# The merge of three branches by features, and chosen remainders for the places of tiles

## The chip, the cores and the metric

The kernel runs on one core of one Trainium2 chip. The metric is the device time of one execution in microseconds. Three runs of the kernel before gave 543.06, 543.06 and 543.47 us, so the median is 543.06 us.

## The reference

One decoder block over 256 positions of 1,024 features, in fp32. A normalised input `h` goes through one wide matrix `w_in`, whose columns feed three token mixers side by side: an attention with compressed, selected and windowed keys (NSA, 16 heads of 64), a chunked linear recurrence (mLSTM, 4 heads of 128) and an attention over 256 fixed memory tokens (4 heads of 128). Three more stretches of 1,024 columns are gates. The branches are merged, projected, normalised and added; a SwiGLU mixer with 2,816 hidden features follows.

```
gm = jax.nn.sigmoid(g_merge.reshape(B, S, N_BRANCH, D_MODEL))
y = (gm[:, :, 0] * (y_nsa @ w_proj_nsa[l]) + gm[:, :, 1] * (y_ml @ w_proj_ml[l])
     + gm[:, :, 2] * (y_mem @ w_proj_mem[l]))
x = x + rmsnorm(y @ w_out[l], g_post_mix[l])
h = rmsnorm(x, g_pre_ffn[l])
gu = h @ w_ffn_in[l]
gate, up = gu[..., :D_FF], gu[..., D_FF:]
x = x + rmsnorm((jax.nn.silu(gate) * up) @ w_ffn_down[l], g_post_ffn[l])
```

## The kernel before

**Split operands.** Each fp32 operand of the large products is split into two parts, `hi` (rounded by the scalar engine, ACT) and `lo` (what is left, by the vector engine, DVE); `split` does it. A product is three matmuls: hi·hi, hi·lo, lo·hi (`mm3`). Weights arrive by DMA in 161 units of 128 x 1,024 fp32 into four buffers `raw`, and `parts` splits each into `whi` and `wlo`, four buffers each. One unit feeds 6,144 streamed columns: 12 matmuls of 512 or 24 of 256.

**Two ways to multiply.** In a matmul one operand is *held* in the array (128 columns, loaded by a weight load) and the other is *streamed* through it.
- *Features-major* (`fmaj`, `fpair`): the weights are held, the activations streamed, 256 columns (the positions) a matmul. The result has features on partitions and tokens along the row. The held tile is used in the order hi, hi, lo and the streamed one in the order hi, lo, hi.
- *Tokens-major* (`tmaj`): the activations are held, the weights streamed, 512 columns a matmul; the result has tokens on partitions.
- `fcat` (gate and up projections of the channel mixer): the weights are held; seven matmuls stream `hi` and `lo` of the activation together, 512 columns, with `hi` weights, then eight stream 256 columns with `lo` weights, then the eighth of 512.

**Stages.** Memory keys and values (`mem_k`, `mem_v`, from the tiles `mh`, `ml`); the normalised input into `hh`, `hl`; keys and values of NSA (`kv`); the small gates (`pgf`); memory attention; then four NSA groups (`nsa_queries`, `nsa_half`), among which other work is placed as filler by the list `ORDER`: `q` and `s` (mLSTM queries and keys), `v`, `g`, `h` (heads), `f`, and six `m`. Each `m` is a `merge_half`: half of the columns of one gate, tokens-major, copied from PSUM into `gm`. After the last group comes the merge. For each half of the features and each branch it takes the sigmoid of `gm`, multiplies the projection in PSUM with it and adds the products in the tile `mrg` on DVE. The sum has tokens on partitions, and `w_out` needs features there, so sixteen transposes of 128 x 128 on the matrix engine bring it to PSUM (`pty`), and `split` writes `yh` and `yl`. Then `w_out`, the first four hidden tiles by `ffn_gate` and `ffn_up` tokens-major, the rest by `fcat`, and `ffn_down`, which holds `u0` to `u5`.

**The order of the work.** Nothing is issued as it is written down. Each operation is recorded with its dependencies (`Plan.record`) and an estimated cost (`cost`); `schedule` lists them onto the engines, `replay` times the list, and `choose` tries two values of a matmul's surcharge, two of slack, and 40 random changes, and keeps the shortest. All DMAs go through the queue of SyncE (SP).

**Where tiles lie.** A tile has its address, in bytes along the partition, from the order in which pools and tags come into use; nothing is chosen. The addresses of the compiled program before, modulo 0x100:

| tile (tag) | used as | address, remainder |
|---|---|---|
| `xc` and the NSA keys `kk` (KK) | streamed | 0x7ac0: 0xc0 |
| `mh`, `u0`, a gate (G, first) | streamed / held | 0xbcc0: 0xc0 |
| `ml`, `u2`, a gate (G, second) | streamed / held | 0xdcc0: 0xc0 |
| `u1`, a gate (G, third) | held | 0x1bd00: 0 |
| `vs`, `u5`, a `wq` (V) | held / streamed | 0xfd00: 0 |
| `ymem`, `yml`, two more (E) | held | 0x11d00, 0x13d00: 0 |
| `hh`, `hl`, later `yh`, `yl` | streamed and held | 0x15d00, 0x17d00: 0 |
| `kmem`, `ynh`, `ynl`, `u3`, `u4` (Y) | streamed / held | 0x1dd00, 0x1fd00: 0 |
| `qs`, `qm` (qs) | held | 0x21d00, 0x22d00: 0 |
| `whi`, `wlo` (four each) | held and streamed | 0x23d00 and on: 0 |
| `pTh`, `pTl` (pT0, pT1) | streamed | 0x33ee0, 0x34f00: 0xe0, 0 |
| `vcs` (held), `ce0`, `ce1` (streamed) | | 0x7240: 0x40; 0x36100, 0x36b00: 0 |

All instructions carry line 598 in the profile, the line that issues the recorded operations, so groups are told apart by the names of tiles.

Of the kernel before, what the change touches and what calls it, by code (L numbers as in the profile page):

```python
# [168 lines left out]
class Plan:  # L169
# [67 lines left out]
    @staticmethod  # L237
    def cost(op):

        n = op.outs[0].n if op.outs else 0  # L240
        views = op.outs + op.ins
        sources = [v for v in op.ins if not v.tile.psum and v.n > 1]
        wide = op.method in ("tensor_copy", "tensor_scalar") and not any(v.tile.psum for v in op.outs)
        op.port = op.eng == "POOL" and bool(op.ins) or op.eng == "DVE" and len(sources) > 1 - wide
        op.load = 0.0
        if op.dma:
            n = views[0].n * 4
            return views[0].shape[0] * n / (230.0 if n < 2048 else 400.0)
        if op.eng == "PE":
            dtype = op.a[1].dtype  # L250
            op.load = 56.0 if dtype == BF16 else 109.0
            if op.method == "transpose":
                return n / 1.2 + 2
            if dtype == F32:
                return max(1.72 * op.a[1].n, n / 0.6 + 10)
            return n / 2.4 + (2.5 if dtype == BF16 else 13.3) + (100 if op.a[1].shape[0] <= 32 else 0)
        n = max(v.n for v in views)
        psum = any(v.tile.psum for v in views)
        pointers = sum(v.n == 1 for v in op.ins)
        part = any(v.place() != (0, P) and v.shape[0] >= 32 for v in op.outs + [v for v in op.ins if v.n > 1])  # L260
# [12 lines left out]
        return 100 + 1.4 * n if op.method == "tensor_scalar" else max(150.0, 2.1 * n - 70)  # L273
# [80 lines left out]
    def schedule(self, matmul, slack, boost):  # L354
# [50 lines left out]
        while len(order) < len(ops):  # L405
# [123 lines left out]

    MATMUL, SLACK, PASSES, ROUNDS = (10.0, 13.3), (60.0, 130.0), 3, 40  # L530

    def choose(self):
# [51 lines left out]
        return self.schedule(matmul, slack, boost)  # L584

    def issue(self):
        order = self.choose()
# [3 lines left out]
        arg = lambda x: x.real() if isinstance(x, View) else x  # L591
        with self.tc.manual_schedule():
            for op in order:
# [4 lines left out]
                op.ins_ = getattr(op.real, op.method)(*map(arg, op.a), **{k: arg(x) for k, x in op.kw.items()})  # L598
# [3 lines left out]
def block_kernel(ctx, tc, order, xN, xT, memN, head, cst, vec, row, wg, w1, w2, W, out):  # L602
# [55 lines left out]

    def parts(raw, into=None):
        hi, lo = into or [wpool.tile([P, 1024], F32R, tag=t, bufs=4, name=t) for t in ("whi", "wlo")]  # L660
        split(hi, lo, raw)
        return hi, lo

    def unit(key, into=None):
        if key not in ready:
            fetch(key)
        return parts(ready.pop(key), into)

# [13 lines left out]
    def fcat(xc, w, ps):  # L682


        hi, lo = unit(w)
        b = lambda k: slice(k * P, (k + 1) * P)
# [13 lines left out]

    def tmaj(xs, *key, n=4, ps_new=ps_d, into=None, last=0):

# [13 lines left out]
        for u in range(n - last):  # L716
            w = unit((*key, u))
            for tb in range(2):
                use(u, tb, w)
        us = range(n - last, n)  # L720
        ws = [unit((*key, u), into and into[u]) for u in us]
        for tb in range(2):
# [61 lines left out]
    wgt = work.tile([P, 1024], F32, tag="p", bufs=2, name="wgt")  # L784
    w2t = one.tile([P, 192], F32, name="w2t")
    part(0, 776)
# [9 lines left out]
    for u in range(4):  # L796
        if u and ("mem_k", u) not in ready:
            fetch(("mem_k", u))
        raw = ready.pop(("mem_k", u)) if u else mt[:, 264:1288]
        w = [wpool.tile([P, 1024], F32R, tag=t, bufs=4, name=t) for t in ("whi", "wlo")]  # L800
        pieces = HEAD[u]
# [38 lines left out]

    vps = tmaj(M, "mem_v", ps_new=ps_s)
    with plan.later(60):
# [30 lines left out]

    hid = one.tile([P, 2, NG, 32], F32, name="hid")
    POOL.memset(hid, 0.0)
    for j in range(2):
# [20 lines left out]
        bias = work.tile([P, 1], F32, tag="b1", bufs=2, name="cbias")  # L897
        DVE.tensor_copy(bias, ph[:, 64:65])
# [198 lines left out]
    def ml_head(h):  # L1097
# [60 lines left out]

    gm = [bigt("G", 3, [P, 2, D], F32, f"gm{b}") for b in range(3)]
# [121 lines left out]
    yl = bigt("hl", 1, [P, 8, S], F32R, "yl")  # L1281
    for h in range(2):
        c = slice(512 * h, 512 * h + 512)
        m = [work.tile([P, 1024], F32, tag="p", bufs=2, name="mrg") for _ in range(2)]
        for b, name, xs, n in ((1, "proj_ml", yml, 2), (2, "proj_mem", ymem, 2), (0, "proj_nsa", (ynh, ynl), 4)):
            g2 = gm[b][:, :, c]
            ACT.activation(g2, g2, AF.Sigmoid, after=last_exp)
            for tb, ps in enumerate(tmaj(xs, name, h, n=n, ps_new=ps_ds, last=2)):
                acc, new = m[tb][:, 0:512], m[tb][:, 512:1024]
                if b == 1:  # L1290
                    DVE.tensor_mul(acc, ps, gm[b][:, tb, c])
                else:
                    DVE.tensor_mul(new, ps, gm[b][:, tb, c])
                    DVE.tensor_add(acc, acc, new)
# [128 lines left out]
def _layout(inputs):  # L1423
# [110 lines left out]
```

## Time and profile before

| | |
|---|---|
| median of three runs | 543.06 us |
| span of the profiled execution, first to last instruction | 540.7 us |
| what lies around it (543.06 − 540.7) | 2.4 us |
| matrix engine busy | 530.9 us, 3,116 matmuls |
| DVE busy | 414.2 us |
| ACT busy | 340.8 us |
| mean granted clock of the matrix engine | 0.999 |
| DMA | 97.85 MB, mean 181 GB/s |

The profile is one execution on the chip. A row that groups instructions gives the busy time, the mean length of one and the idle time of the engine ahead of them. Matmuls are pipelined and the ends of their rows are modelled, so lengths overlap (a matmul of 512 columns is shown as 389 ns long while the next one begins 227 ns after it). What a matmul costs in a run without waits is therefore read from one start to the next.

### The profile page before, as it was taken

What the parts mean: (1) busy time and instruction counts of PE and PEld (TensorE: products, weight loads), DVE (VectorE), ACT (ScalarE), POOL (GpSimd) and SP (SyncE); (2) the same over time, 40 slices, a digit from 0 to 9 for tenths busy, and PEclk for the clock granted to TensorE, in tenths of its full rate; (3) what the DMA queues carried; (4) which work ended last, traced back from release to release, by engine and by line L of the source; (5) the groups of instructions that cost most, each with busy time, mean ns of one, the idle gap of its engine ahead of it and who ended that gap; (6) DMA issues with size and microseconds to landing.
All of it is one profiled execution on the core that took longest, in us unless ns stands there. A gap on an engine that the chain in (4) does not pass through costs nothing.

```text
span 540.7 us, 8802 instructions
## 1 busy us (share of the span) xinstructions
PE 530.9 (98%) x3116; PEld 464.9 (86%) x3116; DVE 414.2 (77%) x900; ACT 340.8 (63%) x682; POOL 30.2 (6%) x43
## 2 busy tenths in 40 slices
PE   9999999999999999999999999999999999999995
PEld 9899998998989889888888888788888888888884
DVE  6795696799999998997987796965777777754543
ACT  7695695566688885966895435744555556653431
POOL 0110000010010111101120000000000000000000
PEclk9999999999999999999999999999999999999999
DMA  8995346525433264254455474834455555555512
GB/s 317 416 412 188 129 136 195 183 79 199 146 137 128 88 234 155 98 177 155 149 174 187 167 257 159 272 118 156 166 190 189 193 196 195 189 187 191 190 63 78
DMA packets 28699, 97.85 MB, mean 181 GB/s; under 512 B 3312, under 2 KB 5232, under 8 KB 28400
## 3 DMA queue, kind: packets, MB, share of 16 engines
q1 hardware_dynamic: 28656, 97.30, 50.6%
q8 instruction: 24, 0.39, 0.3%
q14 instruction: 19, 0.16, 0.1%
HBM read 95.19 MB, written 1.05 MB: 178 GB/s over the span
## 4 chain that ended last, share of the span: by engine, by line
PE 79%; DVE 9%; ACT 5%; DMA 4%; issue 2%; POOL 1%; SPq 0%; DVEq 0%; ACTq 0%
PE pd L598 41%; PE pss L598 27%; DMA raw<-in_W 4%; DVE wlo L598 2%; PE pvn L598 2%; PE sc L598 2%; ACT whi L598 1%; PE ptn L598 1%; PE ph L598 1%; DVE cy L598 1%; ACT L598 1%; DVE sc L598 1%; DVE xt L598 1%; PE psm L598 1%; PE pgf L598 1%
## 5 line engine op out<-in xcount | busy, mean ns | idle before, releaser
L598 DVE TENSOR_TENSOR wlo<-raw,whi 128x1024 fp32r<-128x1024 f32 (+1 forms) x159 | 191.7, 1210 | 83.8 <-ACT whi L598 82.4
L598 ACT ACTIVATE whi<-raw 128x1024 fp32r<-128x1024 f32 (+1 forms) x159 | 166.2, 1051 | 128.8 <-PE pd L598 64.7
L598 PE MATMUL pd<-hh,whi 128*128 128x256 f32 x208 | 59.4, 286 | 0.9 <-DVE on L598 0.9
L598 PE MATMUL pd<-hh,wlo 128*128 128x256 f32 x208 | 59.5, 286 | 0.0
L598 PE MATMUL pd<-hl,whi 128*128 128x256 f32 x208 | 59.2, 285 | 0.0
L598 PE MATMUL pd<-whi,hh 128*128 128x512 f32 x144 | 57.7, 400 | 0.0
L598 PE MATMUL pd<-wlo,hh 128*128 128x512 f32 x144 | 57.5, 399 | 0.0
L598 PE MATMUL pd<-whi,hl 128*128 128x512 f32 x144 | 57.0, 398 | 0.0
L598 PE MATMUL pss<-xc,whi 128*128 128x512 f32 x168 | 43.6, 395 | 0.0
L598 PE MATMUL pss<-whi,u 128*128 128x512 f32 x132 | 42.0, 390 | 0.0
L598 PEld LDWEIGHTS pd<-hh,whi 128*128 128x128 f32 x208 | 39.7, 191 | 1.3 <-DVE on L598 1.1
L598 PEld LDWEIGHTS pd<-hh,wlo 128*128 128x128 f32 x208 | 39.8, 191 | 0.0
L598 PEld LDWEIGHTS pd<-hl,whi 128*128 128x128 f32 x208 | 39.7, 191 | 0.1
L598 PEld LDWEIGHTS pss<-xc,whi 128*128 128x128 f32 x168 | 30.5, 188 | 5.6
L598 PE MATMUL pd<-xc,whi 128*128 128x512 f32 x120 | 32.2, 397 | 0.0
L598 PEld LDWEIGHTS pd<-whi,hl 128*128 128x128 f32 x144 | 27.1, 188 | 4.4
L598 PEld LDWEIGHTS pd<-whi,hh 128*128 128x128 f32 x144 | 27.1, 188 | 4.4 <-ACT cx L598 0.3
L598 PEld LDWEIGHTS pd<-wlo,hh 128*128 128x128 f32 x144 | 27.1, 188 | 4.3 <-DVE wlo L598 0.3
L598 DVE CUSTOM_DVE_ANT_0 sc<-sc,msk 128x16 f32<-128x16 f32 (+2 forms) x96 | 27.2, 316 | 4.2 <-PE sc L598 3.4
L598 PEld LDWEIGHTS pss<-whi,u 128*128 128x128 f32 x132 | 24.8, 188 | 5.3
L598 ACT ACTIVATE pp<-sc,mx 128x128 f32<-128x128 f32 (+1 forms) x64 | 26.7, 427 | 1.5 <-DVE mx L598 1.3
L598 PE MATMUL pss<-wlo,u 128*128 128x512 f32 x66 | 25.8, 390 | 0.0
(333 smaller groups left out, 1122.0 us busy)
## 6 DMA issues: line engine op xcount, KB each, us to landing
raw<-in_W SPq DMA_DIRECT2D x161, 512.0 KB, 3.4
w<-in_w SPq DMA_DIRECT2D x2, 1024.0 KB, 8.1
xn<-in_xN SPq DMA_DIRECT2D x2, 512.0 KB, 9.8
xt<-in_xT SPq DMA_DIRECT2D x2, 512.0 KB, 8.2
mn<-in_memN SPq DMA_DIRECT2D x2, 512.0 KB, 8.8
kk<-kk SPq DMA_DIRECT2D x8, 128.0 KB, 3.1
x<-in_xN SPq DMA_DIRECT2D x2, 512.0 KB, 3.8
memt<-in_head SPq DMA_DIRECT2D x1, 512.0 KB, 6.4
```

The costliest lines, as they stand in the source:

```text
L598: op.ins_ = getattr(op.real, op.method)(*map(arg, op.a), **{k: arg(x) for k, x in op.kw.items()})
```

## The change

The merge and its gates are computed features-major. `gm` holds features on partitions; a gate comes from `fpair` (12 pairs of feature tiles in the place of six halves tokens-major), the projections from `fmaj`, in four pairs of feature tiles. The sum `acc` then lies as `w_out` needs it, and `split` reads it from SBUF. The weights of the gates and projections are laid out in features-major units by the host; there are 161 units as before.

`lay_out` gives tiles their places: for each pool in turn it takes the tags in the order of `RESIDUE`, adds a pad so that the tag's place has the wanted remainder modulo 0x100, and allocates all other tags behind. `whi` and `wlo` become 1,088 columns wide, and a unit starts 0, 32 or 48 columns into them (0, 0x80 or 0xc0 bytes): 0 for features-major products, 48 for tokens-major ones (0 for `mem_v` and for those units of `ffn_down` that meet `u` tiles in G and V), and 32 for the `hi` part of `fcat`. To make room, `w2t` and `hid` share the tiles `ce0` and `ce1`, `cbias` has one buffer, and the unused result of the mLSTM squares goes to a part of `msk` that is not read any more.

The planner's costs of a plain matmul change from n/2.4 + 13.3 (less 0 or 3.3) to n·17/38.4 + 1.5 (less 0 or 3.0), and it tries 100 random changes instead of 40.

```diff
-            return n / 2.4 + (2.5 if dtype == BF16 else 13.3) + (100 if op.a[1].shape[0] <= 32 else 0)
+            return (n / 2.4 + 2.5 if dtype == BF16 else n * 17 / 38.4 + 1.5) + (100 if op.a[1].shape[0] <= 32 else 0)
...
-                        cost += matmul - 13.3
+                        cost += matmul
...
-    MATMUL, SLACK, PASSES, ROUNDS = (10.0, 13.3), (60.0, 130.0), 3, 40
+    MATMUL, SLACK, PASSES, ROUNDS = (-3.0, 0.0), (60.0, 130.0), 3, 100
...
+    FIRST_BYTE = 0x4080
+    RESIDUE = {"vcs": 0, "V": 0, "C": 0, "G": 0, "qs": 0, "KK": 0xC0, "E": 0xC0, "Y": 0xC0, "hh": 0xC0, "hl": 0xC0,
+               "whi": 0, "wlo": 0, "raw": 0, "pT0": 0xC0, "pT1": 0xC0, "ce0": 0xC0, "ce1": 0xC0}
+
+    def lay_out(self, order):
...
+        place = self.FIRST_BYTE
+        rank = {label: i for i, label in enumerate(self.RESIDUE)}
+        for name in ("one", "big", "wpool", "work"):
+            pool, slots = pools[name]
+            for (label, n), size in sorted(slots.items(), key=lambda x: (rank.get(x[0][0], 99), x[1])):
+                pad = (self.RESIDUE[label] - place) % 0x100 if label in rank else 0
+                if pad:
+                    pool.tiles.tile([P, pad // 4], F32, tag=f"pad{place}", bufs=1, name="pad")
+                pool.tiles.tile([P, (size + 31) // 32 * 8], F32, tag=f"{label}_{n}", bufs=1, name="slot")
+                at[label, n] = place + pad
+                place += pad + (size + 31) // 32 * 32
...
+    def room(shift=(0, 0)):
+        return [wpool.tile([P, 1088], F32R, tag=t, bufs=4, name=t)[:, n:n + 1024] for t, n in zip(("whi", "wlo"), shift)]
...
-        hi, lo = unit(w)
+        hi, lo = unit(w, shift=(32, 0))
...
-    def tmaj(xs, *key, n=4, ps_new=ps_d, into=None, last=0):
+    def tmaj(xs, *key, n=4, ps_new=ps_d, into=None, last=0, shift=lambda u: 48):
...
-    vps = tmaj(M, "mem_v", ps_new=ps_s)
+    vps = tmaj(M, "mem_v", ps_new=ps_s, shift=lambda u: 0)
...
-            junk = work.tile([P, P], F32, tag="junk", bufs=2, name="junk")
-            ACT.activation(junk, num[:, tb, h, :], AF.Square, accum_out=ssq[:, tb, h:h + 1])
+            ACT.activation(msk[:, K_MT - K_M0:], num[:, tb, h, :], AF.Square, accum_out=ssq[:, tb, h:h + 1])
...
-        for tb, ps in enumerate(tmaj(X, "g_merge", b, h, last=2)):
-            ACT.activation(gm[b][:, tb, 512 * h:512 * h + 512], ps, AF.Copy)
+        for p in (2 * h, 2 * h + 1):
+            ACT.activation(gm[b][:, 2 * p:2 * p + 2, :], fpair(X, f"g_merge{b}", p), AF.Copy)
...
-        m = [work.tile([P, 1024], F32, tag="p", bufs=2, name="mrg") for _ in range(2)]
-        for b, name, xs, n in ((1, "proj_ml", yml, 2), (2, "proj_mem", ymem, 2), (0, "proj_nsa", (ynh, ynl), 4)):
-            g2 = gm[b][:, :, c]
-            ACT.activation(g2, g2, AF.Sigmoid, after=last_exp)
-            for tb, ps in enumerate(tmaj(xs, name, h, n=n, ps_new=ps_ds, last=2)):
...
-        for tb in range(2):
-            pt = ps_t([P, 4, P], "pty")
-            for j in range(4):
-                PE.transpose(pt[:, j, :], m[tb][:, j * P:(j + 1) * P], ident)
-            t = slice(tb * P, (tb + 1) * P)
-            split(yh[:, 4 * h:4 * h + 4, t], yl[:, 4 * h:4 * h + 4, t], pt)
+    for p in range(4):
+        c = slice(2 * p, 2 * p + 2)
+        m = work.tile([P, 2, 2, S], F32, tag="p", bufs=2, name="mrg")
+        acc, new = m[:, 0], m[:, 1]
+        for b, name, xs in ((1, "proj_ml", yml), (2, "proj_mem", ymem), (0, "proj_nsa", (ynh, ynl))):
+            if p % 2 == 0:
+                g2 = gm[b][:, 2 * p:2 * p + 4, :]
+                ACT.activation(g2, g2, AF.Sigmoid, after=last_exp)
+            ps = ps_ds([P, 2, S])
+            wu = unit((name, p)) if b else None
+            for j in range(2):
+                if b:
+                    fmaj(ps[:, j, :], xs, range(4), wu, 4 * j)
+                else:
+                    fmaj(ps[:, j, :], xs, range(8), unit((name, 2 * p + j)))
+            if b == 1:
+                DVE.tensor_mul(acc, ps, gm[b][:, c, :])
+            else:
+                DVE.tensor_mul(new, ps, gm[b][:, c, :])
+                DVE.tensor_add(acc, acc, new)
+        split(yh[:, c, :], yl[:, c, :], acc)
...
-    for tb, r in scaled("ffn_down", (Hidden(0), Hidden(1)), KF // 2, ((go, [z2[:, 0, :], z2[:, 1, :]]),), halves(rfd), halves(rf), True):
+    for tb, r in scaled("ffn_down", (Hidden(0), Hidden(1)), KF // 2, ((go, [z2[:, 0, :], z2[:, 1, :]]),), halves(rfd), halves(rf), True,
+                        shift=lambda u: 48 * (tags[u // 2][0] == "Y")):
```

More of the change, by code (lines that the diff above doesn't have):

```diff
@@ L584, in choose @@
         return self.schedule(matmul, slack, boost)
+    FIRST_BYTE = 0x4080
+    RESIDUE = {"vcs": 0, "V": 0, "C": 0, "G": 0, "qs": 0, "KK": 0xC0, "E": 0xC0, "Y": 0xC0, "hh": 0xC0, "hl": 0xC0,
+               "whi": 0, "wlo": 0, "raw": 0, "pT0": 0xC0, "pT1": 0xC0, "ce0": 0xC0, "ce1": 0xC0}
+    def lay_out(self, order):
+        pools, at = {}, {}
+        for op in order:
+            for t in op.tiles:
+                if not t.psum:
+                    slots = pools.setdefault(t.pool.name, (t.pool, {}))[1]
+                    key = t.label, t.place
+                    n = t.n * (2 if t.dtype == BF16 else 4)
+                    slots[key] = max(slots.get(key, 0), n)
+        place = self.FIRST_BYTE
[9 more added lines that the diff above has]
+                place += pad + (size + 31) // 32 * 32
+        self.at, self.end = at, place
     def issue(self):
@@ L592, in issue @@
         with self.tc.manual_schedule():
+            self.lay_out(order)
             for op in order:
@@ L657, in fetch, with parts, unit @@
         return raw
-    def parts(raw, into=None):
-        hi, lo = into or [wpool.tile([P, 1024], F32R, tag=t, bufs=4, name=t) for t in ("whi", "wlo")]
+    def room(shift=(0, 0)):
+        return [wpool.tile([P, 1088], F32R, tag=t, bufs=4, name=t)[:, n:n + 1024] for t, n in zip(("whi", "wlo"), shift)]
+    def parts(raw, into=None, shift=(0, 0)):
+        hi, lo = into or room(shift)
         split(hi, lo, raw)
         return hi, lo
-    def unit(key, into=None):
+    def unit(key, into=None, shift=(0, 0)):
         if key not in ready:
             fetch(key)
-        return parts(ready.pop(key), into)
+        return parts(ready.pop(key), into, shift)
     def mm3(out, ah, al, bh, bl, start, stop, **kw):
@@ L716, in tmaj @@
         for u in range(n - last):
-            w = unit((*key, u))
+            w = unit((*key, u), shift=(shift(u),) * 2)
             for tb in range(2):
@@ L720, in tmaj @@
         us = range(n - last, n)
-        ws = [unit((*key, u), into and into[u]) for u in us]
+        ws = [unit((*key, u), into and into[u], (shift(u),) * 2) for u in us]
         for tb in range(2):
@@ L784, in block_kernel @@
     wgt = work.tile([P, 1024], F32, tag="p", bufs=2, name="wgt")
-    w2t = one.tile([P, 192], F32, name="w2t")
+    w2t = work.tile([P, 192], F32, tag="ce0", bufs=1, name="w2t")
     part(0, 776)
@@ L799, in block_kernel @@
         raw = ready.pop(("mem_k", u)) if u else mt[:, 264:1288]
-        w = [wpool.tile([P, 1024], F32R, tag=t, bufs=4, name=t) for t in ("whi", "wlo")]
+        w = room()
         pieces = HEAD[u]
@@ L871, in block_kernel @@
     MC, MT = [msk[:, 384 + 16 * i:400 + 16 * i] for i in range(2)], mtb
-    hid = one.tile([P, 2, NG, 32], F32, name="hid")
+    hid = work.tile([P, 2, NG, 32], F32, tag="ce1", bufs=1, name="hid")
     POOL.memset(hid, 0.0)
@@ L896, in block_kernel @@
             PE.matmul(ph, w1t[j][:, l, :], st[:, 2 * l % 16, n:n + 80], start=(l == 0), stop=(l == 15))
-        bias = work.tile([P, 1], F32, tag="b1", bufs=2, name="cbias")
+        bias = work.tile([P, 1], F32, tag="b1", bufs=1, name="cbias")
         DVE.tensor_copy(bias, ph[:, 64:65])
@@ L903, in block_kernel @@
     pgf = ps_s([P, S], "pgf")
-    gw = [wpool.tile([P, 1024], F32R, tag=t, bufs=4, name="gw") for t in ("whi", "wlo")]
+    gw = room()
     split(gw[0], gw[1], wgt)
@@ L1156, in ml_finish @@
             split(yml[0][:, :, t], yml[1][:, :, t], pt)
-    gm = [bigt("G", 3, [P, 2, D], F32, f"gm{b}") for b in range(3)]
+    gm = [bigt("G", 3, [P, KD, S], F32, f"gm{b}") for b in range(3)]
     def merge_half(i):
         b, h = i % 3, i // 3
-        for tb, ps in enumerate(tmaj(X, "g_merge", b, h, last=2)):
-            ACT.activation(gm[b][:, tb, 512 * h:512 * h + 512], ps, AF.Copy)
+        for p in (2 * h, 2 * h + 1):
+            ACT.activation(gm[b][:, 2 * p:2 * p + 2, :], fpair(X, f"g_merge{b}", p), AF.Copy)
     def nsa_queries(g):
@@ L1315, in block_kernel, with scaled @@
     DVE.tensor_mul(gp[:, 1, :], g1, gp[:, 0, :])
-    def scaled(name, xs, n, gz, scale, pre, root=False):
+    def scaled(name, xs, n, gz, scale, pre, root=False, **kw):
         ss = work.tile([P, 2, 2], F32, tag="ss", bufs=2, name="ss")
@@ L1323, in scaled @@
             c = slice(512 * h, 512 * h + 512)
-            for tb, ps in enumerate(tmaj(xs, name, h, n=n, ps_new=ps_ds, last=4 * h)):
+            for tb, ps in enumerate(tmaj(xs, name, h, n=n, ps_new=ps_ds, last=4 * h, **kw)):
                 sq = work.tile([P, 512], F32, tag="sq", bufs=3, name="sq")
@@ L1458, in _layout @@
     for b in range(3):
-        for h in range(2):
-            c = C_MG + 1024 * b + 512 * h
-            add_t("g_merge", w_in[:, c:c + 512], b, h)
+        add_f(f"g_merge{b}", w_in, tiles(C_MG + 1024 * b, 8))
+    add_f("proj_nsa", a["w_proj_nsa"][0], tiles(0, 8))
+    for b in ("proj_ml", "proj_mem"):
+        for p in range(4):
+            units[b, p] = np.concatenate([blocks(a["w_" + b][0], slice(c, c + P)).reshape(P, 512)
+                                          for c in (256 * p, 256 * p + P)], axis=1)
     for h in range(2):
-        for b in ("nsa", "ml", "mem"):
-            add_t("proj_" + b, a["w_proj_" + b][0][:, 512 * h:512 * h + 512], h)
         add_t("w_out", a["w_out"][0][:, 512 * h:512 * h + 512], h)
```

7 lines of the change are left out of this document (removed).

## The prediction

> **What bounds the kernel now.** I read the page first, then its chain, then the who-waited-for-whom view of the matrix engine alone.
>
> ```profile
> span 540.7 us, 8802 instructions
> PE 530.9 (98%) x3116; PEld 464.9 (86%) x3116; DVE 414.2 (77%) x900; ACT 340.8 (63%) x682; POOL 30.2 (6%) x43
> PE 79%; DVE 9%; ACT 5%; DMA 4%; issue 2%; POOL 1%; SPq 0%; DVEq 0%; ACTq 0%
> ```
> ```profile
> PE warm L598 <- POOL mhalf L598: 1.0, 1, 1.0
> PE pd L598 <- DVE on L598: 0.9, 1, 0.9
> PE pss L598 <- ACT xc L598: 0.5, 1, 0.5
> PE ptx L598 <- DVE xg L598: 0.3, 1, 0.3
> PE pvn L598 <- POOL ce L598: 0.3, 1, 0.3
> PE rbc L598 <- POOL rm L598: 0.2, 1, 0.2
> ```
>
> The matrix engine is busy for 98% of the span and its named waits add up to 3.2 us. So what counts is how many columns it streams and how long each matmul takes. A duration on the page has a modelled end, so I read the step from one start to the next in the timeline. Its columns are start in us, length, engine, and what was done. First the features-major runs of early projections (256 columns streamed from hh and hl, weights held):
>
> ```profile
> 43.13 0.28 PE L598 MATMUL pd<-hh,wlo 128*128 128x256 f32 x1
> ...
> 46.00 0.28 PE L598 MATMUL pgf<-hh,gw 128*128 128x256 f32 x1
> ```
> There are 24 matmuls from the first row to the last: 2.87 us / 24 = 119.6 ns a step. The same width elsewhere, from mh and ml, and from xc:
>
> ```profile
> 9.06 0.62 PE L598 MATMUL pd<-ml,whi 128*128 128x256 f32 x4
> ...
> 11.34 0.38 PE L598 MATMUL pd<-mh,whi 128*128 128x256 f32 x1
> ```
> ```profile
> 401.53 2.02 PE L598 MATMUL pd<-xc,whi 128*128 128x512 f32 x8
> 403.39 1.07 PE L598 MATMUL pd<-xc,wlo 128*128 128x256 f32 x8
> 404.30 0.39 PE L598 MATMUL pd<-xc,whi 128*128 128x512 f32 x1
> ```
> The first fence has 20 steps in 2.28 us, 114.0 ns each. In the second, 8 steps of 256 columns take 0.91 us, 113.8 ns each, and the 8 of 512 columns before them 1.86 us, 232.5 ns each. So equal work has two prices, 119.6 and about 114. What differs is the place: in the program before, hh, hl and the split weights all begin at a multiple of 256 bytes, while mh, ml and xc begin 0xc0 past one. I call the remainder of the streamed address minus that of the held one, modulo 0x100, the offset: 0 costs 119.6 ns, 0xc0 about 114. The 512-wide tokens-major runs have their own pair:
>
> ```profile
> 481.66 0.39 PE L598 MATMUL pss<-wlo,u 128*128 128x512 f32 x1
> ...
> 484.38 0.39 PE L598 MATMUL pss<-wlo,u 128*128 128x512 f32 x1
> ...
> 485.06 0.39 PE L598 MATMUL pss<-wlo,u 128*128 128x512 f32 x1
> ...
> 488.49 0.39 PE L598 MATMUL pss<-wlo,u 128*128 128x512 f32 x1
> ```
> Between the first two rows lie 12 steps (u1, offset 0): 2.72 us / 12 = 226.7 ns. Between the last two lie 15 (u2, whose place is 0xc0 past, so offset 0x40): 3.43 / 15 = 228.7 ns. The xc runs above with 232.5 ns are 512 wide at offset 0xc0. For 512 columns 0 is cheapest, for 256 columns 0xc0.
>
> **The change, part by part.** The new places give hh, hl, KK, E, Y and the pT tiles remainder 0xc0, and V, C, G, qs and unshifted weights 0. The streamed columns in all stay: the gates' 288 matmuls of 512 become 576 of 256, the projections' 192 become 384; fetched units and splits are as many as before. I sum against the 540.7 us span; 543.06 − 540.7 = 2.4 us lie around it and I leave them as they are.
>
> A. *Existing features-major matmuls.* 696 stream hh or hl (kv, gates, qk_ml, q_mem, q_nsa) at offset 0 and get 0xc0: 696 × (119.6 − 114.0) = **−3.9 us**. Bounds: −4.4 if each comes to 113.3 (half the 226.7 above), −2.0 if half of them, mixed with attention work, do not gain. Rows of the forms (busy us, mean ns, idle before) speak to such mixing:
>
> ```profile
> L598 PE MATMUL pd<-hh,wlo 128*128 128x256 f32 x208 | 59.5, 286 | 0.0
> L598 PE MATMUL pd<-whi,hh 128*128 128x512 f32 x144 | 57.7, 400 | 0.0
> L598 PE MATMUL pss<-xc,wlo 128*128 128x256 f32 x168 | 22.6, 277 | 0.0
> L598 PE MATMUL pvn<-pTl,vs 128*128 128x256 f32 x48 | 12.6, 286 | 0.0
> L598 PE MATMUL pd<-whi,ynh 128*128 128x512 f32 x24 | 9.3, 389 | 0.0
> L598 PE MATMUL psm<-kmem,qm 128*128 128x256 f32 x24 | 3.5, 283 | 0.0
> ```
> The hh form has a mean 9 ns above that of xc,wlo; 5.6 of it is the offset, 3 the mixing.
>
> By the Trainium skill, "TensorE: Matmul & The Clock Gate", section "Back-to-back issue gap", 256 columns take 262 cycles, 109.2 ns; by that figure A would be an estimated 696 × 10.4 = 7.2 us. No run of 256-wide steps quoted here shows less than 113.8, so the sum does not use it.
>
> B. *Sixteen transposes of the merge go* (mrg to pty, four groups of four).
>
> ```profile
> 301.88 0.60 PE L598 MATMUL pty<-cs,mrg 128*128 128x128 f32 x4
> 302.24 0.48 PE L598 MATMUL pss<-whi,ymlt 128*128 128x512 f32 x1
> 302.55 0.40 PE L598 MATMUL pss<-wlo,ymlt 128*128 128x512 f32 x1
> ```
> From the group's start until the matmul behind it is done are 0.67 us; less its own 0.227 that is 0.44 us a group, four groups **−1.8 us**. It lay on the matrix engine, which has no slack there, so it all counts. The split that followed reads the sum from SBUF instead of PSUM, same count and size. Behind the last one, w_out needs the last pair only for its units' last quarter; 36 matmuls × 227 ns = 8.2 us are ahead of that, against a chain of multiply, add, copy and subtract:
>
> ```profile
> L598 DVE TENSOR_TENSOR mrg<-mrg x8: 684/691/693, 289.7 to 327.4; 128x512 f32<-128x512 f32 x8
> L598 ACT ACTIVATE yh<-pty x4: 579/598/601, 303.2 to 329.4; 128x512 fp32r<-128x512 f32 x4
> ```
> Three DVE steps of 0.69 and one of 0.60 are 2.7 us, so it is hidden. Without that cover it would cost those 2.7 us once.
>
> C. *Gates and projections by features.* In clean stretches 512 at 226.7 and two of 256 at 114.0 are equal within 1.3 ns. In the mixed stretch the form whi,hh has 400 ns against 389 of whi,ynh, about 10 ns more, × 288 gate matmuls = 2.9 us; at 3 ns of mixing, 576 narrow ones carry 1.7. The difference is −1.2, but part of the 10 ns is the neighbouring transposes, which stay; I take half, **−0.6 us**. Bounds: −2.9 (no mixing cost left) and +2.3 (each narrow one 9 ns up, like pTl: 5.2 − 2.9).
>
> D. *Gate and up projections of the channel mixer.* 36 blocks of 8 wide and 8 narrow; hi moves to offset 0x40, lo stays at 0xc0. If it steps like the 0x40 row: 36 × 8 × (232.5 − 228.7) = **−1.1 us**. Bounds: −1.7 (226.7 each), and +0.2: no gain, and the one narrow step a block that now precedes a hi load goes to 119.6. The trace has no narrow step at 0x40.
>
> E. *Runs at 0x40 that go to 0*: mem_v 48, u0 and u2 96, xc over Y and E weights and up 84 = 228 × 2.0 = **−0.5 us** (−0.5 to 0).
>
> F. *mem_k loses.* mh and ml lie in G, which goes to 0: 96 × 5.6 = **+0.5 us**. The opening waits for DMA in part, so 0 to +0.6.
>
> G. psm (283 ns, 24 of them, kmem in Y, held qm at 0) gains 24 × 5.6 = **−0.1 us**; pvn, also new to 0xc0, −0.3 to 0, taken as 0.
>
> H. *The planner's order.* Its costs of a plain matmul hardly move (256 columns: 116.7 or 120 before, 111.8 or 114.8 now; measured 114), and it tries 100 orders instead of 40. The order will be another one. I take 0; the 3.2 us of named waits could shrink by 2 or double. Junk squares now land in a spent part of msk on ACT itself, and w2t and hid share tiles first used much later, so I cost both at nothing: ACT is idle for 37% of the span, which covers a late square. Without that cover the head behind it would wait, and the dearest such wait now is the 0.9 us above.
>
> Sum: −3.9 − 1.8 − 0.6 − 1.1 − 0.5 + 0.5 − 0.1 = −7.5 us. Span 533.2, time 543.06 − 7.5 = **535.6 us**.
>
> **The rivals.**
>
> *R1, the step belongs to the order of operands, not to the place: slower.* Features-major runs hold hi twice and alternate two streamed tiles, which the runs of mh and of xc do not; the psm form (283) alternates too and is dear. Then the 960 new narrow matmuls cost 119.6 each against 113.3: +6.0 us, less 1.8 for the transposes, and A, D, E and F vanish: 547.3 us. Over the 1,656 narrow matmuls it decides from a mean step of 117.0 ns: (960 × 113.3 + 696 × 119.6 + 1,770) / 1,656. Against it: wide steps too differ (226.7, 228.7, 232.5) with one order of u streams and only the tile's place changed.
>
> The Trainium skill supports R1's premise: the same page, section "Step-by-step: what each phase is for", says the engine has two independent SBUF read ports and that loading the next weights doesn't steal bandwidth from the running matmul. By that rule no place could matter; the 226.7 and 228.7 of u1 and u2 disagree with it.
>
> *R2, the pads do not produce the offsets.* If the pools place tiles otherwise, offsets are as mixed as before and the transposes alone go, 541.3 us. For: nothing in the diff compares the place computed with the place given. Against: before, the first tile is at 0x4080 and tiles follow one another in order of first use.
>
> *R3, the vector engine takes over in attention, or the new order waits more.* By stage (us, then busy of PE, PEld, DVE, ACT, POOL):
>
> ```profile
> 140.00:160.00 20.00, 19.12 (x117) 16.35 (x116) 19.47 (x54) 16.37 (x32) 2.79 (x3) 1.00 0.31 109
> 160.00:180.00 20.00, 19.99 (x137) 17.97 (x136) 18.40 (x66) 18.43 (x59) 0.00 (x0) 1.00 0.29 106
> 180.00:200.00 20.00, 20.00 (x111) 17.01 (x111) 18.93 (x65) 15.87 (x47) 3.93 (x3) 1.00 0.54 193
> ```
> DVE is busy for 56.8 of 60 us there; 2 to 3% off PE leaves it almost none. If A's share in this stretch (49 × 5.6 = 0.3) and C (0.6) are given back and the named waits grow by two thirds (2.1), 3.0 us are lost: 538.6 us. Against: the planner can move gate work out of these stages.
>
> **How the numbers follow.** Forecast 0.72, R3 0.17, R2 0.06, R1 0.05. Within the forecast, A to E at their bounds and the order's waits move it by some 3 us each way: 532.6 to 538.6. With R3 and its spread the range is 531.8 to 540.0; R1, R2 and the far tails stay out. A measurement of this kernel tells about 0.2% (1.1 us) from no change: faster than 542.0 are the forecast, nearly all of R3 and most of R2, 0.91; same 0.04; slower 0.05.
>
> **What would show it.** Narrow hh steps in quiet stretches of 113 to 115 ns, and mem_k's at about 119 (A and F; R1 if hh stays at 119); no pty (B); gm written from narrow matmuls that step below 117 on average (C); blocks of xc of 2.74 instead of 2.77 us (D); u0 and u2 at 226.7 (E). I am wrong if hh stays near 119.6, or if the matrix engine's waits exceed 6 us.

## The result and the profile after

The changed kernel takes 537.81 us (median of four runs, 536.69 to 539.94) against 543.06 us. The ratio is 0.9907, with a 95% interval of 0.9882 to 0.9932. It is faster, by 5.25 us where 7.5 were forecast; 535.6 was the forecast and 531.8 to 540.0 its range. The profiled execution took 536.69 us, its span is 534.9 us, 5.8 less than before.

The page of the changed kernel, with its span, the busy times, the chain that ended last by engine and the chain by line; all recorded operations now carry line 627:

```profile
span 534.9 us, 9738 instructions
PE 525.3 (98%) x3580; PEld 482.7 (90%) x3580; DVE 412.9 (77%) x900; ACT 342.1 (64%) x682; POOL 30.6 (6%) x43
PE 85%; DVE 6%; DMA 4%; ACT 2%; issue 1%; SPq 0%; DVEq 0%; ACTq 0%
PE pd L627 44%; PE pss L627 30%; DMA raw<-in_W 3%; PE pvn L627 2%; PE sc L627 2%; DVE wlo L627 2%; PE ptn L627 1%; PE ph L627 1%; DMA gp<-in_row 1%; DVE cy L627 1%; ACT whi L627 1%; DVE wq L627 1%; PE pn L627 1%; PE pvm L627 1%; PE psm L627
```

The matrix engine is still the bound: 98% busy, and 85% of the chain against 79% before. It runs 464 matmuls more (480 from the narrow gates and projections, less the 16 transposes) in 5.6 us less. One entry of the chain is new, `DMA gp<-in_row`; it comes back below. The waits of the matrix engine, in us, times and longest:

```profile
PE warm L627 <- POOL mhalf L627: 1.0, 1, 1.0
PE pss L627 <- ACT xc L627: 0.8, 1, 0.8
PE pd L627 <- ACT whi L627: 0.5, 1, 0.5
PE ptx L627 <- DVE xg L627: 0.3, 1, 0.3
PE sc L627 <- ACT pp L627: 0.2, 1, 0.2
```

They add up to 2.8 us (3.2 before; 3.8 in a second profile of the changed kernel, run again below). No wait has become large. The steps, read as in the prediction from one start to the next, in the matrix engine's timeline of the changed kernel:

```profile
9.72 0.64 PE L627 MATMUL pd<-ml,whi 128*128 128x256 f32 x4
...
12.12 0.64 PE L627 MATMUL pd<-mh,whi 128*128 128x256 f32 x4
...
44.84 0.28 PE L627 MATMUL pgf<-hh,whi 128*128 128x256 f32 x1
...
47.56 0.28 PE L627 MATMUL pd<-hh,whi 128*128 128x256 f32 x1
...
305.19 0.28 PE L627 MATMUL pss<-ynh,whi 128*128 128x256 f32 x1
...
308.59 0.28 PE L627 MATMUL pss<-ynh,whi 128*128 128x256 f32 x1
...
396.43 2.00 PE L627 MATMUL pd<-xc,whi 128*128 128x512 f32 x8
398.26 1.07 PE L627 MATMUL pd<-xc,wlo 128*128 128x256 f32 x8
399.17 0.39 PE L627 MATMUL pd<-xc,whi 128*128 128x512 f32 x1
...
473.10 0.39 PE L627 MATMUL pss<-wlo,u 128*128 128x512 f32 x1
...
484.66 0.40 PE L627 MATMUL pss<-wlo,u 128*128 128x512 f32 x1
```

- `mem_k` (now offset 0): 20 steps in 2.40 us, 120.0 ns; it was 114.0.
- The small gates from `hh`, `hl` (now 0xc0): 24 steps in 2.72 us, 113.3 ns; such a run was 119.6.
- The projections: 30 steps in 3.40 us, 113.3 ns.
- `fcat`: eight wide steps in 1.83 us, about 229 ns (232.5 before), eight narrow in 0.91, 113.8, as before. A block is 2.74 us.
- `ffn_down`: 51 steps in 11.56 us, 226.7 ns.

In quiet stretches, then, every place does what the prediction said.

### The profile page after: what moved, and what is told of

It reads as the page before. It is cut to its first block, busy times and chain, and to the rows that moved or that the text cites. A ratio compares the mean times of both kernels' runs of the same rounds, so it can differ in the third digit from the quotient of the medians.

```text
span 534.9 us, 9738 instructions
## 1 busy us (share of the span) xinstructions
PE 525.3 (98%) x3580; PEld 482.7 (90%) x3580; DVE 412.9 (77%) x900; ACT 342.1 (64%) x682; POOL 30.6 (6%) x43
## 4 chain that ended last, share of the span: by engine, by line
PE 85%; DVE 6%; DMA 4%; ACT 2%; issue 1%; SPq 0%; DVEq 0%; ACTq 0%
PE pd L627 44%; PE pss L627 30%; DMA raw<-in_W 3%; PE pvn L627 2%; PE sc L627 2%; DVE wlo L627 2%; PE ptn L627 1%; PE ph L627 1%; DMA gp<-in_row 1%; DVE cy L627 1%; ACT whi L627 1%; DVE wq L627 1%; PE pn L627 1%; PE pvm L627 1%; PE psm L627 1%
## 5 line engine op out<-in xcount | busy, mean ns | idle before, releaser
L627 PE MATMUL pd<-hh,whi 128*128 128x256 f32 x400 | 113.7, 284 | 0.1
L627 PE MATMUL pd<-hh,wlo 128*128 128x256 f32 x400 | 112.7, 282 | 0.0
L627 PE MATMUL pd<-hl,whi 128*128 128x256 f32 x400 | 112.4, 281 | 0.0
L627 PEld LDWEIGHTS pd<-hh,whi 128*128 128x128 f32 x400 | 75.3, 188 | 0.4 <-DVE on L627 0.3
L627 PEld LDWEIGHTS pd<-hl,whi 128*128 128x128 f32 x400 | 75.6, 189 | 0.1
L627 PEld LDWEIGHTS pd<-hh,wlo 128*128 128x128 f32 x400 | 75.3, 188 | 0.0
L627 PEld LDWEIGHTS pd<-xc,whi 128*128 128x128 f32 x120 | 21.9, 188 | 3.5
L627 PEld LDWEIGHTS pss<-xc,wlo 128*128 128x128 f32 x168 | 22.3, 188 | 1.8
L627 PE MATMUL pss<-xc,wlo 128*128 128x256 f32 x168 | 22.6, 277 | 0.0
L627 DVE TENSOR_SCALAR pp<-pp,sm 128x256 f32<-128x256 f32 (+1 forms) x72 | 19.6, 316 | 0.1
```

## The experiments

A study that splits the change comes first: the planner alone, the places alone, the merge by features alone, and the changed kernel with one place put back. The kernels give the tiles in PSUM longer names (`p_` or `t_` and the weights), so rows can be told apart; nothing else follows from that. The planner's kernel and the merge alone are built on the kernel before, so their rows have line 598. Times are medians; each ratio is to the kernel before in runs beside it. Where only places differ (`hh` and `hl` put back or at 0x80, `mem_k` and `fcat` moved), every engine's instructions stand in the same order as in the kernel that was edited, so order can't explain those rows.

| kernel | us | ratio to before, 95% |
|---|---|---|
| planner alone | 542.18 | 0.9999 (0.9990 to 1.0009) |
| places, merge tokens-major | 536.2 | 0.9888 (0.9872 to 0.9903) |
| merge by features, places of before | 544.74 | 1.0044 (1.0029 to 1.0059) |
| changed, `hh` and `hl` at remainder 0 | 542.78 | 1.0006 (0.9996 to 1.0015) |
| changed kernel again | 538.03 | 0.9922 (0.9908 to 0.9937) |
| places, again | 536.61 | 0.9899 (0.9886 to 0.9913) |
| places, transposes left out | 535.67 | 0.9881 (0.9866 to 0.9896) |
| places, `mem_k` weights 16 columns on | 536.13 | 0.9896 (0.9882 to 0.9910) |
| changed, gains row loaded early | 536.12 | 0.9883 (0.9868 to 0.9898) |
| changed, `hh` and `hl` at 0x80 | 541.98 | 0.9988 (0.9978 to 0.9998) |
| places, `fcat`'s `hi` weights 48 columns on | 538.2 | 0.9921 (0.9906 to 0.9936) |

**The planner alone.** The kernel before with the new costs and 100 random changes:

```diff
-            return n / 2.4 + (2.5 if dtype == BF16 else 13.3) + (100 if op.a[1].shape[0] <= 32 else 0)
+            return (n / 2.4 + 2.5 if dtype == BF16 else n * 17 / 38.4 + 1.5) + (100 if op.a[1].shape[0] <= 32 else 0)
...
-    MATMUL, SLACK, PASSES, ROUNDS = (10.0, 13.3), (60.0, 130.0), 3, 40
+    MATMUL, SLACK, PASSES, ROUNDS = (-3.0, 0.0), (60.0, 130.0), 3, 100
```

> The kernel before with only the planner's new costs and its 100 random changes. Theory P (the place of the streamed tile against the held one sets the step of a matmul): no step changes, so 543.1 us within about 1.5 us for another order of the same work; narrow steps over hh stay at 119.6 ns. Rival H (the gain is the planner's): 540 us or less.

Measured: 542.18 against 542.27 us. The planner gives nothing by itself; step H holds.

**The places alone.** The changed kernel, its gates and merge tokens-major as before, transposes included:

```diff
-            ACT.activation(gm[b][:, 2 * p:2 * p + 2, :], fpair(X, f"g_merge{b}", p), AF.Copy)
+        for tb, ps in enumerate(tmaj(X, "g_merge", b, h, last=2)):
+            ACT.activation(gm[b][:, tb, 512 * h:512 * h + 512], ps, AF.Copy)
...
+            for j in range(4):
+                PE.transpose(pt[:, j, :], m[tb][:, j * P:(j + 1) * P], ident)
```

> The changed kernel with the merge and the gates tokens-major as before: planner, places and shifts alone. Theory P: 696 narrow steps over hh and hl go from 119.6 to 113 to 118 ns (-3.1 us), the wide ones over xc from 232.5 to about 229 (-0.9), mem_k goes up (+0.5): 539 us. Rival R1 (the order of the operands makes the step): the steps over hh stay at 119.6 and the time at 543 us.

Measured: 536.2 us, 6.1 below the kernel before beside it. The places alone give all that the whole change gives, and rather more. The expectation said 539. Of the 5.9 us between the span of the planner's kernel and this one, 2.9 are the narrow steps over `hh` and `hl` and 0.9 is `fcat`, as expected; 1.6 more lie in `pvn` (17.19 to 15.55 us), half of it a wait for the vector engine that this order of the work doesn't have.

**The merge alone.** The planner's kernel with the gates and the merge by features, places as before:

```diff
+            ACT.activation(gm[b][:, 2 * p:2 * p + 2, :], fpair(X, f"g_merge{b}", p), AF.Copy)
...
-                PE.transpose(pt[:, j, :], m[tb][:, j * P:(j + 1) * P], ident)
...
+        split(yh[:, c, :], yl[:, c, :], acc)
```

> The kernel before with the planner's new costs and with the merge and gates by features, but no chosen places: hh, E, Y and the weights all at remainder 0. Theory P: 960 narrow matmuls at 119.6 in the place of 480 wide ones at 226.7 to 230 cost some 5 us, the sixteen transposes give 1.8 back: 546 us. If the merge by features gains by itself: 541 us.

Measured: 544.74 us, slower by 0.44%. At offset 0 two narrow steps cost 12.5 ns more than a wide one (2 × 119.6 − 226.7). With 480 wide ones replaced that would be 6.0 us, less the transposes; 2.6 us more than the planner's kernel is what came. In the traces of these two kernels the gates cost 3.0 us more and the projections 2.3, the transposes give 1.4 back, and 1.5 are gained in `pvn`, 0.8 of them a wait that is gone.

**One place put back.** The changed kernel, with `hh` and `hl` at remainder 0:

```diff
-    RESIDUE = {"vcs": 0, "V": 0, "C": 0, "G": 0, "qs": 0, "KK": 0xC0, "E": 0xC0, "Y": 0xC0, "hh": 0xC0, "hl": 0xC0,
+    RESIDUE = {"vcs": 0, "V": 0, "C": 0, "G": 0, "qs": 0, "KK": 0xC0, "E": 0xC0, "Y": 0xC0, "hh": 0, "hl": 0,
```

> The changed kernel with the places of hh and hl (yh and yl too) at remainder 0 in the place of 0xc0 and nothing else changed. Theory P: 1,272 narrow steps come to 119.6 ns from a mean of 115.7 (+4.8 us), and 240 wide ones that hold hh or yh come to 232 ns (+1.3): 544 us. Rival R1: no step changes, 537.8 us.

Measured: 542.78 us. Two numbers in a table of places take back the whole gain. Part of it goes through wide steps: tokens-major products over the same tiles move to offset 0xc0, where their quiet steps are 233 ns. In the matrix engine's groups by form the mean of one (last column but one) shows where; here the kernel with the merge alone, the one with `hh` put back, and the changed kernel again, in this order:

```profile
L598 PE MATMUL p_g_merge<-hh,whi 128*128 128x256 f32 x192 | 55.1, 287 | 0.0
L598 PE MATMUL p_proj_nsa<-ynh,whi 128*128 128x256 f32 x64 | 18.1, 283 | 0.0
```
```profile
L627 PE MATMUL p_g_merge<-hh,whi 128*128 128x256 f32 x192 | 55.2, 288 | 0.0
...
L627 PE MATMUL p_proj_nsa<-ynh,whi 128*128 128x256 f32 x64 | 18.0, 281 | 0.0
```
```profile
L627 PE MATMUL p_g_merge<-hh,whi 128*128 128x256 f32 x192 | 54.6, 285 | 0.0
...
L627 PE MATMUL p_proj_nsa<-ynh,whi 128*128 128x256 f32 x64 | 17.7, 276 | 0.0
```

The projections go from 283 to 276 with the new places, 7 ns; the gates from 287 to 285, 2 ns, though both change their offset from 0 to 0xc0. And with `hh` put back the projections, whose tiles did not move, lose most of it (281). This is the first sign that the place isn't all; the section on the prediction returns to it.

**The changed kernel and the places once more, beside each other.** No edit but the names:

```diff
-    def ps_ds(shape):
+    def ps_ds(shape, name="pds"):
```

> The changed kernel itself, with names of PSUM tiles that tell the gates and projections apart. Theory M (the merge by features has given its transposes back: the gates' narrow steps, mixed with attention, cost 0.6 us more than the wide ones did, and the waits at the end of w_out grew): no faster than the kernel with places alone, ratio to it 0.999 to 1.003. Theory of the prediction (transposes and gates gain 2.4 us over places alone): ratio 0.9955.

> Planner, places and shifts alone (merge tokens-major, with its sixteen transposes) again, beside the changed kernel on the same chip. Both theories: 536 to 538 us, 0.989 of the kernel before.

Measured: 538.03 and 536.61 us. Given the new places, the merge by features costs 1.4 us, between 0.2 and 0.3%; the intervals of the two ratios overlap by 0.0005, so the sign is likely rather than certain. In the two profiles, whose spans are 535.2 and 535.4 us, the transposes' 1.4 us are gone, but the steps of `w_out`, waits included, add up to 24.26 us instead of 22.65; what more the medians show has no owner there.

**The transposes left out.** The places alone, where the split reads the sum as it lies:

```diff
-            pt = ps_t([P, 4, P], "pty")
-            for j in range(4):
-                PE.transpose(pt[:, j, :], m[tb][:, j * P:(j + 1) * P], ident)
+            pt = m[tb][:, 0:512].rearrange("p (j t) -> p j t", j=4)
```

> Places alone, and the sixteen transposes of the merge left out: the split reads the untransposed sums, so the rows of y go to wrong places, and all else stays. If the transposes lie on the bound (step B of the prediction): 1.8 us less than places alone. If the time they free turns into a wait elsewhere: less than 0.7 us less.

Measured: 535.67 against 536.61 us with them. From the last `pvn` to the start of `w_out` the trace has 38.70 us instead of 39.97: sixteen transposes are worth 1.3 us there, 0.9 in the medians (the intervals of the two ratios overlap), not 1.8.

**`mem_k` at 0xc0.** The places alone, `mem_k`'s weights 16 columns (0x40) into their tiles:

```diff
-        w = room()
+        w = room((16, 16))
```

> Places alone, and the split weights of mem_k begin 16 columns (0x40 bytes) later, so that its streamed tiles stand at offset 0xc0 again. Theory P: 96 steps go from 119.9 back to 114 ns, 0.5 us less in the trace's opening. If the opening waits for its DMAs anyway: the steps fall and the time does not.

Measured: 536.13 against 536.61 us; quiet steps of `mem_k` fell from 119.8 to 113.6 ns. 96 of them are worth 0.6 us; the intervals of the two ratios overlap nearly whole, and the profiled span did not shrink (535.7 against 535.4). In the opening the matrix engine now waits 1.3 us for `whi` from ACT instead of 0.4, and ACT itself waits there for weights from DMA (1.0 and 1.3 us for `raw`): the steps fell and a wait took their place.

**The gains row loaded early.** Which new wait cost the merge its gain? The trace of the changed kernel, run again, has the row of gains `gp` (of `g_pre_ffn`), the trace before has it too; the view is that of one tile, with durations in ns and first and last start in us, then what its users waited for. First before, then the changed kernel:

```profile
L598 DVE TENSOR_TENSOR xg<-x,gp x2: 1220/1221/1222, 317.2 to 321.7; 128x1024 f32<-128x1024 f32 x2
...
L598 SPq DMA_DIRECT2D gp<-in_row x1: 327/327/327, 310.1 to 310.1; - x1
```
```profile
L627 DVE TENSOR_TENSOR xg<-x,gp x2: 1215/1220/1226, 318.2 to 322.2; 128x1024 f32<-128x1024 f32 x2
L627 SPq DMA_DIRECT2D gp<-in_row x1: 328/328/328, 313.0 to 313.0; - x1
...
  DMA gp<-in_row: 1.0, 1
```

`gp` takes a buffer of the gates (tag G, three). Merged by features, each gate is read until the last of the four pairs; the buffer comes free later, the load is issued at 313.0 us instead of 310.1 (305.6 with the places alone), and DVE waits 1.0 us for it before `xg` (0.5 in the first profile, where the load is issued at 313.6). The experiment gives the row a tile of its own, in the place of `kk` and `xc`, which is unused at that time:

```diff
-    for t, i in ((g1, 520), (gp[:, 0, :], 520 + 2 * D), (go, 520 + D)):
+    gk = bigt("KK", 1, [P, D], F32, "gk")
+    for t, i in ((g1, 520), (gk, 520 + 2 * D), (go, 520 + D)):
```

> The changed kernel, with the row of gains g_pre_ffn loaded into the place of the NSA keys, free after the last group, in the place of a gate's tile that comes free only in the merge's last quarter. Theory L (that late load holds up the DMA queue and the vector engine, and this is the longer wait at the end of w_out): no wait for the row, the two waits at the end of w_out under 1.0 us together (1.4 and 2.2 in the two profiles of the changed kernel), 536.5 us. If the late load is covered: waits as they were, 537.8 us.

Measured: 536.12 us, ratio 0.9883 (0.9868 to 0.9898), against 0.9922 (0.9908 to 0.9937) and 0.9907 (0.9882 to 0.9932) without the edit. The row, in the view of its tile:

```profile
L627 DVE TENSOR_TENSOR xg<-x,gk x2: 1219/1220/1221, 314.7 to 320.4; 128x1024 f32<-128x1024 f32 x2
L627 SPq DMA_DIRECT2D gk<-in_row x1: 328/328/328, 264.9 to 264.9; - x1
```

From the start of `w_out` to `fcat` the trace has 46.96 us, against 48.59 in the changed kernel's second profile and 47.71 in its first. The waits of the matrix engine behind `w_out`, in the second profile of the changed kernel and in this one (`t_ffn_gat` is the gate product of the first hidden tiles, named `pss` above):

```profile
PE t_ffn_gat L627 <- ACT xc L627: 1.0, 1, 1.0
PE ptx L627 <- DVE xg L627: 0.9, 1, 0.9
```
```profile
PE ptx L627 <- DVE xg L627: 0.3, 1, 0.3
PE t_ffn_gat L627 <- DVE xc L627: 0.3, 1, 0.3
```

That is 1.9 against 0.6 us; the first profile of the changed kernel had 1.1 (0.3 and 0.8, shown above), the places alone 0.3 and 0.4. So the late row was a new wait of the merge, and with it gone the waits behind `w_out` are shorter than in both profiles of the changed kernel. How the row's 0.5 to 1.0 us before `xg` at 318 us come out as waits after 341 us no view here follows step by step, and the two profiles of one kernel differ by 0.8 us in these waits. This version is faster than the kernel before, with the lowest ratio of all that do the whole work, and isn't told apart from the places alone (0.9883 and 0.9888). Its interval lies clear of the changed kernel's second measurement and overlaps that of the first.

**`hh` and `hl` at 0x80.** The changed kernel, with the weights of tokens-major products moved so that these keep offset 0:

```diff
-    RESIDUE = {"vcs": 0, "V": 0, "C": 0, "G": 0, "qs": 0, "KK": 0xC0, "E": 0xC0, "Y": 0xC0, "hh": 0xC0, "hl": 0xC0,
+    RESIDUE = {"vcs": 0, "V": 0, "C": 0, "G": 0, "qs": 0, "hh": 0x80, "hl": 0x80, "KK": 0xC0, "E": 0xC0, "Y": 0xC0,
...
-    def tmaj(xs, *key, n=4, ps_new=ps_d, into=None, last=0, shift=lambda u: 48):
+    def tmaj(xs, *key, n=4, ps_new=ps_d, into=None, last=0, shift=lambda u: 32):
```

> The changed kernel with hh, hl, yh, yl at remainder 0x80 in the place of 0xc0, and the tokens-major shifts for them at 32 so that the wide steps keep offset 0. 1,272 narrow steps stand at offset 0x80, which no trace has shown in quiet. Theory P: a level of their own; with the two levels of 0xc0 (113.3 and 117.7) kept, 537.8 us; at 119.6, 543 us; all at 113.3, 535.5 us. Wide steps over hh unchanged, about 229 ns.

Measured: 541.98 us, 0.9988. The timeline of the matrix engine has 24 steps of the small gates in 2.85 us, 118.6 ns from the unrounded starts, nearly what offset 0 costs:

```profile
44.73 0.28 PE L627 MATMUL pgf<-hh,whi 128*128 128x256 f32 x1
...
47.58 0.28 PE L627 MATMUL p_q_mem<-hh,whi 128*128 128x256 f32 x1
```

**`fcat`'s wide steps at offset 0.** The places alone, `hi` 48 columns into its tile instead of 32:

```diff
-        hi, lo = unit(w, shift=(32, 0))
+        hi, lo = unit(w, shift=(48, 0))
```

> Places alone (merge tokens-major), and the hi weights of the channel mixer begin 48 columns in, so that the wide steps over xc stand at offset 0 in the place of 0x40. Theory P by the tokens-major rows (226.7 at 0, 228.7 at 0x40): wide steps of 226.7 to 227, one narrow step a block up to 120; 0.5 us less than places alone. If wide steps at 0 after narrow ones fall into a dearer state, as those over hh did in the mixed stretch (230): no gain.

Measured: 538.2 us, ratio 0.9921, slower than the 0.9888 and 0.9899 of the same kernel without the edit (its interval lies clear of the first's and overlaps the second's by 0.0007). Neither branch of the expectation came. The timeline of the matrix engine:

```profile
396.73 1.11 PE L627 MATMUL pds<-xc,wlo 128*128 128x256 f32 x8
397.68 2.00 PE L627 MATMUL pds<-xc,whi 128*128 128x512 f32 x8
399.51 1.11 PE L627 MATMUL pds<-xc,wlo 128*128 128x256 f32 x8
```

The starts shown are rounded; over all 36 blocks the narrow steps now take 117.7 ns on the mean instead of 114.2, though their own addresses did not change, and the wide ones 230.7 instead of 230.5: offset 0 made them no cheaper. A block has 2.78 us instead of 2.74, and all 36 have 101.1 us instead of 100.0. What a step costs depends on what ran before it, not on its own two addresses alone.

## Why the prediction was right, and where it was off

The kernel is bound by the matrix engine's steps, the places set the step, and the forecast's direction and the mechanism of the places stand: places alone give 6.1 us (5.4 when measured again), one place put back takes everything back. The other half of the change did not do what was forecast: B and C together were to give 2.4 us, and beside the places alone the merge by features costs 1.4. That the total still fell in its range is partly luck: the places gave 5.4 to 6.1 us where A, D, E, F and G add up to 5.1.

Part by part, from the starts of all matmuls of a part in the two profiles (a wait counts to the part in which it stands):

| step | forecast, us | measured, us | from |
|---|---|---|---|
| A, existing runs over `hh`, `hl` | −3.9 | −3.1 | `kv` 24.43 to 23.36, `q_mem` 11.76 to 11.20, `q_nsa` 23.58 to 22.90, `qk_ml` 23.39 to 22.72, small gates 2.88 to 2.72 |
| B, transposes | −1.8 | −1.4 | their own steps before, 1.42; 1.3 with them left out |
| C, gates and projections | −0.6 | −0.15 | gates 69.05 to 69.63; projections 44.34 to 43.61, 0.5 of it a wait of `pvn` for `ce` |
| D, `fcat`, wide steps | −1.1 | −0.95 | 67.27 to 66.33; narrow 114.0, unchanged |
| E, runs from 0x40 to 0 | −0.5 | −0.2 | `ffn_up` 10.99 to 10.90, `ffn_down` 59.86 to 59.78, `mem_v` −0.05 |
| F, `mem_k` | +0.5 | +0.9 | 12.30 to 13.17, 0.5 of it a wait for `whi` |
| G, `psm` | −0.1 | −0.16 | 2.88 to 2.72 |
| G, `pvn` | 0 | −1.3 | 16.70 to 15.40, 0.9 of it a wait for `on` that went |
| not in the forecast: `sc` | 0 | +0.7 | 12.61 to 13.35, 0.2 of it a wait |
| H, waits of the engine | 0 | −0.4, in the rows above and in `w_out` | named waits 3.2 to 2.8 |

Without H, whose waits stand in other rows, the measured column adds up to −5.7 us; the difference of the two spans is −5.8. Where the 1.7 us went that the forecast has more, is then: A 0.8, B 0.4, C 0.45, D 0.15, E 0.3, F 0.4 and `sc` 0.7 fell short, 3.1 in all before rounding; `pvn` gave 1.3 more than forecast, and small parts 0.1. Most of what `pvn` gave is a wait that the new order of the work does not have, which the forecast had not counted on: luck again. (The profiled execution was the shortest of four, so the medians differ by 5.25 only.) This accounting is worked out from two profiles. The two profiles of the changed kernel differ by 0.5 us in `mem_k` and by 0.9 in `w_out`, where waits stand, and by up to 0.3 us in the parts without large waits.

**A and C: the step has two levels.** The prediction took about 114 ns as the price of a narrow step at 0xc0, and 5.6 ns as what each of the 696 gains. In the quiet run quoted above that is what it got (113.3). In the stretch where attention, mLSTM and gates are mixed it is not so. Two runs of the changed kernel's timeline, less than 6 us apart, same tiles, same offsets:

```profile
208.08 0.28 PE L627 MATMUL pd<-hh,whi 128*128 128x256 f32 x1
...
209.14 0.28 PE L627 MATMUL pd<-hh,whi 128*128 128x256 f32 x1
...
213.40 0.28 PE L627 MATMUL pd<-hl,whi 128*128 128x256 f32 x1
...
215.55 0.28 PE L627 MATMUL pd<-hh,wlo 128*128 128x256 f32 x1
```

Nine steps in 1.06 us are 117.8 ns, nineteen in 2.15 us are 113.2. The step has a level, and keeps it: take the narrow steps at 0xc0 of the large products that another narrow matmul follows and that last 110 to 120 ns. Of 1,626 adjacent pairs of them in this profile 1,073 are both short (under 115.5 ns), 484 both long, 67 go from long to short (36 of these at the start of a block of `fcat`) and 2 from short to long. A run begins long or short, and a long one may fall later. About half of the steps over `hh` and `hl` (559 of 1,139) were long, and 559 × 4.4 ns = 2.5 us is what the long ones cost. So in A the failing term is "696 × (119.6 − 114.0)": its price was read in a quiet run, and −3.1 lies between it and the bound of −2.0 for half of the steps not gaining. In C it is the "3 ns of mixing": the mean of the three gate forms, 283.7 in the changed kernel's second profile, is 7.7 above the 276 of the projections. The gates alone lost 0.6 us, against the forecast sign; the projections gained 0.7.

**B.** The prediction had 0.44 us a group; with the transposes left out, 1.3 us went, 0.32 a group. Read from its own steps before, a group has 0.36. The prediction followed the chain behind the last sum into `w_out` and found it hidden, which no wait here contradicts. What it left out is who waits for the gates' buffers. Features-major, all three stay in use to the end of the merge, and the row of gains that needs one of them is late. This cost stands in none of its steps; the row loaded early points to it, with the limits said there.

**D, E, F, G.** D's eight wide steps went to about 229 as the row at 0x40 had said. E was over-sized: `ffn_down`, 59.86 us before from its first start to its last, had only 0.25 above 263 steps of 226.67 ns (59.61), and 0.2 of 0.5 us came. F's steps rose to 120.0 as forecast; beyond that the part has a wait of 0.5 us for `whi` that the profile before doesn't have, and putting its steps back to 113.6 moved no time.

**The rivals.** *R1, order of operands:* refuted. Order is the same in the quoted runs of 119.6 and 113.3 ns, and a remainder alone moved the kernel by some 5 us. The rule of the Trainium skill that stood behind it ("TensorE: Matmul & The Clock Gate", section "Step-by-step: what each phase is for": two independent SBUF read ports, loading the next weights takes no read bandwidth from the running matmul), read as the prediction reads it, that no place could matter, disagrees with the kernel with `hh` put back. There only places differ, and the narrow steps over `hh` and `hl` of 110 to 122 ns have a mean of 119.4 instead of 115.6 ns. The measurement decides. *R2, pads without effect:* refuted by the same rows. *R3:* its 538.6 us is nearer to 537.81 than the forecast's 535.6, but its first half did not happen. The windows that the prediction quoted read now (us, then busy of PE, PEld, DVE, ACT, POOL):

```profile
140.00:160.00 20.00, 19.92 (x126) 17.28 (x125) 18.56 (x40) 16.62 (x26) 2.68 (x2) 1.00 0.34 116
160.00:180.00 20.00, 20.00 (x174) 19.75 (x173) 18.65 (x70) 19.07 (x67) 0.47 (x1) 1.00 0.43 149
180.00:200.00 20.00, 20.00 (x176) 20.00 (x175) 18.73 (x68) 16.11 (x41) 4.00 (x3) 1.00 0.47 159
```

DVE is busy for 55.9 of 60 us, less than the 56.8 before, and PE for 59.9: the matrix engine never gave up its place. The named waits shrank in this profile (3.2 to 2.8 us) and grew a little in the second (3.8), far from the 2.1 more that R3 needs. What R3 had right is that A and C would be given back in part in this stretch; the giver, as far as the steps show it, is their level.

## What to carry to other kernels

Where the matrix engine is the bound, measure the step from start to start for each pair of streamed and held tile, and look at the two addresses modulo 0x100: here that alone was worth 1.1%, more than a restructured merge. Take a step's gain from the stretch where it will run, not from the quiet one, and put a large change's parts to the clock one by one: this one held a part that gained nothing beside the places, likely in part through a transfer that came late. When a tile's life gets longer, list the loads that wait for its buffer.

## What the runs showed of the hardware

- In these runs the step follows the streamed address less the held one, modulo 0x100, and differently by width. 256 columns: 119.6 to 120.0 ns at 0, 118.6 at 0x80, 113.3 or 117.7 at 0xc0. 512 columns: 226.7 at 0 (but 230.7 in `fcat`), about 229 at 0x40, 232.5 to 233.3 at 0xc0. That the difference counts, and not one address, rests on `mem_k`: streamed at 0, held at 0x40, it has 113.6 ns like `hh` at 0xc0 with weights at 0.
- At 0xc0 the narrow step has two levels that persist, 113.3 and 117.7 ns. With `hh` put back to 0, or at 0x80, the projections (own offset 0xc0) stay on the long one nearly throughout (374 of 377 steps in either trace). And the small gates over `hh` and `hl`, 113.3 ns in both profiles of the changed kernel, have 117.8 with the gains row loaded early, at the same remainders and with the matrix engine's work in the same order. The timeline of the kernel with `hh` at 0, 40 steps in 4.71 us, 117.8 ns:

```profile
310.19 0.28 PE L627 MATMUL p_proj_nsa<-ynl,whi 128*128 128x256 f32 x1
...
314.90 0.28 PE L627 MATMUL p_proj_nsa<-ynh,wlo 128*128 128x256 f32 x1
```

- In `fcat`, wide steps at 0 ahead put the narrow ones on the long level too (117.7), and wide steps at 0x40 ahead leave them on the short one (113.8). What sets the level is open: no run here isolates it. The Trainium skill ("TensorE: Matmul & The Clock Gate", section "Back-to-back issue gap") gives 262 cycles for 256 columns, 109.2 ns, as the gap of an isolated matmul; the shortest level here is 113.3.
